# Seven products instead of eight: the MLP of a two-layer encoder by Strassen's scheme, with the sums of weight blocks formed on GpSimd

## The chip, the cores and the metric

The kernel runs on one core of a Trainium2 chip. A core has five engines, each with its own queue of instructions that it takes in order: TensorE (PE, matrix products, with its weight loads shown apart as PEld), VectorE (DVE), ScalarE (ACT), GpSimd (POOL) and SyncE (SP, which here only starts transfers). They wait for each other through semaphores. The metric is the time of one launch on the device in microseconds (us). The kernel before takes 1675.76 us (median of three runs, 1674.79 to 1677.36).

## The reference, cut to what matters

Two layers run over 512 prompt tokens and 32 sample tokens, 544 in all, at width 1024. Each layer has two attention mixers, a cross-attention to 256 memory tokens, and a squared-ReLU MLP of width 4096. The change is about the MLP:

```python
D_MODEL = 1024; D_FF = 4 * D_MODEL; DEPTH = 2
...
def layer(x, pos, l, past, mk, mv):
    mix, rows = mixers(rmsnorm(x, norm_mix[l]), pos, l, past)
    x = x + mix
    x = x + cross_attention(rmsnorm(x, norm_cross[l]), mk, mv, w_xq[l], w_xo[l])
    hm = rmsnorm(x, norm_mlp[l])
    x = x + jnp.square(jax.nn.relu(hm @ w_up[l])) @ w_down[l]
    return x, rows
```

All arithmetic is float32. The products are formed from float32 numbers split into a high and a low part (`wh + wl`, `ah + al`), with three products `wl*ah + wh*ah + wh*al` kept of the four.

## The kernel before

Activations lie in SBUF as features by tokens: `X` [128, 8, 544] is the residual stream, `Ah`/`Al` the two parts of the normed input of a product, `Bh`/`Bl` those of the second product's input. A weight matrix is cut into blocks of 128 output features over 1024 input features ([128, 1024] in SBUF, one transfer of 512 KB each). `split_piece` (lines 208 to 229) makes the two parts of half a block [128, 512]: ScalarE copies it to the rounded type `fp32r` (line 222), and VectorE (even halves) or GpSimd (odd halves) subtracts to get the rest (line 224).

`dense` (line 256) makes one block of outputs: over eight blocks of the contraction, `mm3` (line 246) issues three products for each half of the tokens (272 columns each), so 48 matmuls a block, into one of two PSUM tiles `pd` of two banks. The MLP (in `build`) goes in four groups a layer: eight blocks of `w_up`, then eight blocks of `w_down` that use them. `evac_up` (line 1036) takes a block out of PSUM: VectorE computes max(x, 0) times the norm's factor `R` (line 1039), ScalarE squares it to `Bh` (1040), GpSimd squares it in full (1041), and `rest_up` subtracts on VectorE to `Bl` (1045). `evac_x` (line 986) adds a finished block to `X` on VectorE (line 990) and, in the last group, prepares the next norm with a square on ScalarE and a sum `acc` on GpSimd (line 346). The last two blocks of the second layer go by halves of the tokens (`finish`, `final_norm`).

The order of instructions on each engine comes from a scheduler, which takes the program's order as a priority and may put a later instruction ahead; each engine then keeps that order on the chip. The next block's weights are split while a block's products run.

Of the kernel before, what the change touches and what calls it, by code (L numbers as in the profile page):

```python
# [29 lines left out]
# where in each layer's stream of products the other steps come: after how many of the first blocks' products  # L30
# [11 lines left out]
# norm, and evacuation of the first block that needs it  # L42
NORM = (dict(cross=[8, 11], mlp=(9, 10)),
        dict(cross=(9, 10), mlp=(9, 10)))
# the order of the last outputs: blocks, on GpSimd or not
# [3 lines left out]
# columns of the small constant tables  # L49
# [5 lines left out]
GATE = slice(64, 96)  # L55

# [5 lines left out]
class Program:  # L62
    def __init__(self, ctx, tc, io):
        self.ctx, self.tc, self.nc, self.io = ctx, tc, tc.nc, io
        self.order = []
        self.raw = {}
        self.split = {}
        self.n_loaded = 0
        self.n_split = 0

    # ---------------------------------------------------------------- storage
    def setup(self):
# [13 lines left out]
        # the gains and the first block of the input come in one piece  # L86
# [6 lines left out]
        self.Bl = one.tile([128, KT, NT], F32R, name="Bl")  # L93
        self.Rm = one.tile([128, NMEM], F32, name="Rm")
# [45 lines left out]

    def load_x(self, k):
# [55 lines left out]
    # ---------------------------------------------------------------- weights  # L197
    def load_weights(self, upto):
        while self.n_loaded <= min(upto, len(self.order) - 1):
            i = self.n_loaded  # L200
            ap, pieces, _ = self.order[i]
# [6 lines left out]
    def split_piece(self, i, j):  # L208
        nc = self.nc
        self.load_weights(i)  # L210
        _, pieces, spare = self.order[i]
        out = self.split.setdefault(i, [None] * len(pieces))
        if out[j] is not None:
            return
        n = pieces[j]
# [14 lines left out]

    def split_weights(self, upto, part=None):
        """Splits the weights up to the given block; with part, only that many of the last block's pieces."""
        upto = min(upto, len(self.order) - 1)
        while self.n_split <= upto:
            i = self.n_split
# [1211 lines left out]
```

## Time and profile before

| | |
|---|---|
| median of three runs | 1675.76 us |
| profiled execution, first to last instruction | 1676.7 us |
| TensorE matmuls busy | 1639.7 us (98%), 12543 recorded |
| VectorE, ScalarE, GpSimd busy | 764.5, 695.8, 558.4 us (46%, 41%, 33%) |
| share of TensorE in the chain that ended last | 90% |
| transfers | 157.28 MB, mean 94 GB/s |

The page shows no time of the profiled execution beside its span, so the two first rows are the ones to compare. Busy times are unions: matmuls overlap in the pipeline, so the mean of one (288 ns) is longer than the distance between two. The two MLP stages are the stretches from about 464 to 847 us and from 1285 to 1662 us.

### The profile page before, as it was taken

How to read it: one execution, taken by the hardware profiler on the slowest of the kernel's cores; microseconds unless marked ns; L12 is line 12 of the kernel's file. 1: busy time of each engine (PE TensorE's matmuls, PEld its weight loads, DVE VectorE, ACT ScalarE, POOL GpSimd, SP SyncE). 2: the span in 40 equal slices, each digit the busy share in tenths (PEclk: the TensorE clock that was granted, in tenths of full speed). 3: DMA queues.
4: the chain of work that ended last, by engine and by line, in shares of the span. 5: the costliest groups of instructions: out<-in, count | busy, mean ns of one | idle time of the engine just before them, and what ended most of it. 6: DMA issues, size and time to landing. Idle time of an engine off the chain costs nothing.

```text
span 1676.7 us, 30750 instructions
## 1 busy us (share of the span) xinstructions
PE 1639.7 (98%) x12543; PEld 1554.7 (93%) x12543; DVE 764.5 (46%) x1534; ACT 695.8 (41%) x1429; POOL 558.4 (33%) x500
## 2 busy tenths in 40 slices
PE   8899999999999999999999999999999999999997
PEld 7777889998999999999998778999999999999996
DVE  6956674355442322323358656634554323232233
ACT  6645564444432222223446556544444223232233
POOL 4514232421442322323344223333124323232334
PEclk9899999999999999999999999999999999999998
DMA  4313155221322222222223113542222222222222
GB/s 161 98 42 109 59 167 177 82 83 60 96 89 89 88 89 89 88 89 89 85 81 101 68 52 102 160 157 85 72 68 89 89 88 89 89 89 89 88 89 79
DMA packets 56398, 157.28 MB, mean 94 GB/s; under 512 B 6768, under 2 KB 16048, under 8 KB 56256
## 3 DMA queue, kind: packets, MB, share of 16 engines
q1 hardware_dynamic: 55984, 155.02, 29.6%
q8 instruction: 99, 1.62, 0.4%
q14 instruction: 43, 0.35, 0.1%
q10 hardware_dynamic: 272, 0.28, 0.0%
HBM read 143.49 MB, written 11.75 MB: 93 GB/s over the span
## 4 chain that ended last, share of the span: by engine, by line
PE 90%; DVE 4%; DMA 1%; POOL 1%; issue 0%; ACT 0%; SPq 0%; DVEq 0%; POOLq 0%; ACTq 0%
PE pd L254 76%; PE pt L394 1%; PE S L493 1%; PE S L561 1%; PE pv L588 1%; PE pv L447 1%; PE S L492 1%; PE pv L507 1%; PE S L429 1%; DMA sn<-sin 1%; PE pd L897 1%; PE ph L254 1%; POOL sw L665 1%; PE pt L574 0%; DVE wl L224 0%
## 5 line engine op out<-in xcount | busy, mean ns | idle before, releaser
L222 ACT CAST wh<-raw 128x512 fp32r<-128x512 f32 (+1 forms) x488 | 301.0, 618 | 718.0 <-PE pd L254 673.3
L224 POOL TENSOR_TENSOR wl<-raw,wh 128x512 fp32r<-128x512 f32 (+1 forms) x240 | 311.8, 1300 | 664.3 <-ACT wh L222 455.8
L254 PE MATMUL pd<-Ah,wl 128*128 128x272 f32 (+2 forms) x2032 | 458.8, 297 | 6.3 <-DVE wl L224 3.6
L254 PE MATMUL pd<-Ah,wh 128*128 128x272 f32 (+2 forms) x2032 | 440.1, 288 | 1.0 <-ACT Ah L330 0.8
L254 PE MATMUL pd<-Al,wh 128*128 128x272 f32 (+2 forms) x2032 | 439.3, 287 | 0.1
L254 PEld LDWEIGHTS pd<-Ah,wl 128*128 128x128 f32 (+1 forms) x2032 | 327.9, 189 | 18.5 <-issue 9.4
L254 PEld LDWEIGHTS pd<-Ah,wh 128*128 128x128 f32 (+1 forms) x2032 | 327.9, 189 | 2.4 <-ACT Ah L330 1.9
L254 PE MATMUL pd<-Bh,wl 128*128 128x272 f32 x1568 | 328.8, 290 | 0.9 <-DVE qr L648 0.7
L254 PEld LDWEIGHTS pd<-Al,wh 128*128 128x128 f32 (+1 forms) x2032 | 327.2, 188 | 0.5 <-DVE Al L331 0.5
L254 PE MATMUL pd<-Bh,wh 128*128 128x272 f32 x1568 | 325.8, 288 | 0.0
L254 PE MATMUL pd<-Bl,wh 128*128 128x272 f32 x1568 | 325.2, 288 | 0.0
L254 PEld LDWEIGHTS pd<-Bh,wl 128*128 128x128 f32 x1568 | 246.0, 189 | 3.3 <-issue 1.0
L254 PEld LDWEIGHTS pd<-Bh,wh 128*128 128x128 f32 x1568 | 246.3, 188 | 0.5
L254 PEld LDWEIGHTS pd<-Bl,wh 128*128 128x128 f32 x1568 | 246.2, 188 | 0.3
L990 DVE TENSOR_TENSOR XG<-pd,XG 128x544 f32<-128x544 f32 x94 | 68.2, 725 | 362.0 <-PE pd L254 362.0
L224 DVE TENSOR_TENSOR wl<-raw,wh 128x512 fp32r<-128x512 f32 (+1 forms) x248 | 174.7, 705 | 35.7 <-ACT wh L222 35.1
L1039 DVE SCALAR_TENSOR_TENSOR up<-pd,R 128x544 f32<-128x544 f32 x64 | 46.4, 725 | 171.1 <-PE pd L254 170.9
L1041 POOL TENSOR_TENSOR up<-up 128x544 f32<-128x544 f32 x64 | 70.4, 1100 | 145.8 <-ACT Bh L1040 145.8
L346 POOL TENSOR_TENSOR acc<-acc,sq 128x544 f32<-128x544 f32 x47 | 65.9, 1402 | 122.9 <-ACT sq L345 122.8
L1045 DVE TENSOR_TENSOR Bl<-up,Bh 128x544 fp32r<-128x544 f32 x64 | 46.5, 726 | 74.9 <-POOL up L1041 74.9
L372 ACT ACTIVATE P<-P,nm 128x128 f32<-128x128 f32 (+1 forms) x96 | 54.1, 564 | 38.2 <-DVE nm L370 37.3
L379 DVE TENSOR_SCALAR P<-P,ss 128x128 f32<-128x128 f32 (+3 forms) x144 | 65.0, 451 | 3.8
(276 smaller groups left out, 1551.5 us busy)
## 6 DMA issues: line engine op xcount, KB each, us to landing
raw<-w_up SPq DMA_DIRECT2D x64, 512.0 KB, 3.5
raw<-w_down SPq DMA_DIRECT2D x64, 512.0 KB, 3.5
raw<-w_in SPq DMA_DIRECT2D x28, 512.0 KB, 3.5
raw<-w_mk SPq DMA_DIRECT2D x16, 512.0 KB, 3.7
raw<-w_mv SPq DMA_DIRECT2D x16, 512.0 KB, 3.8
raw<-w_out SPq DMA_DIRECT2D x16, 512.0 KB, 3.6
raw<-w_xq SPq DMA_DIRECT2D x16, 512.0 KB, 3.5
raw<-w_xo SPq DMA_DIRECT2D x16, 512.0 KB, 3.6
```

The lines of the kernel that those rows point to most:

```text
L222: nc.scalar.copy(h[:, :n], r)
L224: eng.tensor_tensor(lo[:, :n], r, h[:, :n].bitcast(F32), ALU.subtract)
L254: nc.tensor.matmul(o, w, a[:, c0:c1], start=start and n == 0, stop=stop and n == 2)
L346: nc.gpsimd.tensor_tensor(self.acc, self.acc, sq, ALU.add)
L372: nc.scalar.activation(P[:, :n], P[:, :n], AF.Exp, bias=nm, scale=-1.0, accum_out=ss)
L379: nc.vector.tensor_scalar(P[:rows, :n], P[:rows, :n], ri[:rows], None, ALU.mult)
L394: nc.tensor.transpose(pt[:, j], P[:, j * 128:(j + 1) * 128], self.ident)
L429: nc.tensor.matmul(ps[:, :w], q[hh][:r, i * 128:n], k[hh][:r, :w], start=m == 0, stop=m == 1)
L990: nc.vector.tensor_tensor(x, ps[:, :, :HALF], x, ALU.add)
L1039: nc.vector.scalar_tensor_tensor(halves(t), ps[:, :, :HALF], 0.0, halves(self.R), ALU.max, ALU.mult)
L1041: nc.gpsimd.tensor_tensor(t, t, t, ALU.mult)
L1045: self.nc.vector.tensor_tensor(self.Bl[:, j], self.up.pop(j), self.Bh[:, j].bitcast(F32), ALU.subtract)
```

## The change

The MLP's two products are done by pairs. In `w_up`, a pair is output block j of the group together with block j + 4; in `w_down`, output block i with block i + 4. The contraction is halved (4 blocks each), and the tokens are halved (272 each). That makes a 2 x 2 by 2 x 2 product of blocks, which Strassen's scheme (in Winograd's form) does with seven products for eight. Each product is 4 contraction blocks by 3 parts, 12 matmuls of 272 columns: 84 a pair, where two blocks took 96.

- Weight side (`split_sum`): of the seven factors three are blocks of weights (`W11`, `W12`, `W22`) and four are sums (`S1` to `S4`), each formed on GpSimd, then split as before by ScalarE and by VectorE or GpSimd (`on_pool`: `S3`, `W12`, `W22` while products of `w_up` are issued, `W12`, `W22` else). A pair has seven splits of [128, 512] where two blocks had four.
- Activation side: `G` holds the four blocks and three sums; `parts` splits them into seven slots for each of the four block pairs (`W7`). For `w_up` this is done once a layer (`wide_a`, `wide_b`, during the products of `w_xo`, whose blocks now come in the order `PAIRED`), for `w_down` in each group by `evac_up`.
- Results add up in PSUM: `PRODUCTS` names for each product its slot and one of three banks X, Z, W. Between the products into X and Z the sums so far are read out: by ScalarE copies (`evac_up`, n < 3), or by VectorE additions into `X` (`evac_down`). Product n + 2 into a bank waits until that reading is done.
- Splits are issued four products ahead (`LOOK`); each pair's two transfers of 512 KB go to one of two sets of buffers.

```diff
+B11, TA, B22, TB, TC, B21, TD = range(7)
+W11, S1, S2, S4, S3, W12, W22 = range(7)
+PRODUCTS = ((B11, "X", True), (TA, "Z", True), (TB, "X", False), (B22, "Z", False), (TC, "X", False),
+            (B21, "W", True), (TD, "X", False))
+HP = 4
+LOOK = 4
...
+    def split_sum(self, i, j):
...
+        (w11, w21), (w12, w22) = [(t[:, :512], t[:, 512:]) for t in self.raw[i]]
+        sums = self.sums.setdefault(i, {})
+        if j in (S1, S2, S3, S4):
+            a, b = {S1: (w21, w22), S2: (sums.get(S1), w11), S4: (sums.get(S2), w12), S3: (w11, w21)}[j]
+            sums[j] = self.p_tile()
+            nc.gpsimd.tensor_tensor(sums[j], a, b, ALU.add)
+            r = sums[j]
+        else:
+            r = {W11: w11, W12: w12, W22: w22}[j]
...
+        h, lo = [pool.tile([128, 512], F32R, tag=tag + x, name="w" + x, bufs=3) for x in "hl"]
+        nc.scalar.copy(h, r)
+        eng = nc.gpsimd if j in self.on_pool else nc.vector
+        eng.tensor_tensor(lo, r, h.bitcast(F32), ALU.subtract)
+        return h, lo
...
+    def pair(self, ap, ops, evac):
...
+        def product(n):
+            slot, bank, first = PRODUCTS[n]
...
+            for i in range(HP):
+                c = slice(i * 128, (i + 1) * 128)
+                ah, al = [self.W7[ops + x][i][:, slot] for x in "hl"]
+                for m, (w, a) in enumerate(((lo, ah), (h, ah), (h, al))):
+                    self.nc.tensor.matmul(st[bank], w[:, c], a, start=first and i == 0 and m == 0,
+                                          stop=i == HP - 1 and m == 2, skip_group_check=True)
...
+    def parts(self, ops, i, s):
+        h, lo = [self.W7[ops + x][i][:, s] for x in "hl"]
+        self.nc.scalar.copy(h, self.G[:, s])
+        self.nc.vector.tensor_tensor(lo, self.G[:, s], h.bitcast(F32), ALU.subtract)
+    def sums_a(self, b12):
+        self.nc.vector.tensor_tensor(self.G[:, TA], self.G[:, B11], b12, ALU.subtract)
+    def sums_b(self, b12):
+        nc, G = self.nc, self.G
+        nc.vector.scalar_tensor_tensor(G[:, TB], G[:, TA], -1.0, G[:, B22], ALU.mult, ALU.subtract)
+        nc.vector.tensor_tensor(G[:, TC], G[:, B22], b12, ALU.subtract)
+    def sums_c(self):
+        nc, G = self.nc, self.G
+        nc.vector.scalar_tensor_tensor(G[:, TD], G[:, TB], -1.0, G[:, B21], ALU.mult, ALU.subtract)
...
-    def evac_up(self, j, ps):
-        nc = self.nc
-        t = self.t_tile("up")
-        nc.vector.scalar_tensor_tensor(halves(t), ps[:, :, :HALF], 0.0, halves(self.R), ALU.max, ALU.mult)
-        nc.scalar.activation(self.Bh[:, j], t, AF.Square)
-        nc.gpsimd.tensor_tensor(t, t, t, ALU.mult)
-        self.up[j] = t
...
+    def evac_up(self, j, n, ps):
...
+        if n < 3:
+            nc.scalar.copy(st[n], ps)
+            return
+        def square(out, x, op, t):
+            nc.vector.scalar_tensor_tensor(out, x, 0.0, r[t], op, ALU.mult)
+            nc.scalar.activation(out, out, AF.Square)
+        if n == 3:
+            b = st[3]
+            nc.vector.tensor_tensor(b, ps, st[2], ALU.add)
+            square(b, b, ALU.max, 1)
+        elif n == 4:
+            nc.vector.tensor_tensor(G[:, B22], ps, st[1], ALU.add)
+            square(G[:, B22], G[:, B22], ALU.min, 1)
+        elif n == 5:
+            nc.vector.tensor_tensor(G[:, B11], ps, st[0], ALU.add)
+            square(G[:, B11], G[:, B11], ALU.max, 0)
+            self.sums_a(st[3])
+            self.parts("B", j, slice(B11, TA + 1))
+        if n == (4 if j == HP - 1 else 5):
+            self.sums_b(st[3])
+            self.parts("B", j, slice(B22, TC + 1))
+        if n == 6:
+            square(G[:, B21], ps, ALU.min, 0)
+            self.sums_c()
+            self.parts("B", j, slice(B21, TD + 1))
+    def evac_down(self, i, goff, n, ps):
...
+        x = self.X[:, i + HP * m, h[t]]
+        nc.vector.tensor_tensor(x, x, ps, op)
...
+            self.on_pool = (S3, W12, W22) if p[3] == "A" else (W12, W22)
+            for z in todo[q:q + LOOK + 1]:
+                self.split_piece(*z)
+            p[1](n)
```

Two places show what this puts on the engines. VectorE first, where the second group of the first layer begins. In the kernel before, the last block of `w_down` (`XG<-pd,XG`) is followed by the first block of `w_up` (`up`, `Bl`), with the splits of weights (`wl`) between:

```order
L990 TENSOR_TENSOR XG<-pd,XG 128x544
L224 TENSOR_TENSOR wl<-raw,wh 128x512
L1039 SCALAR_TENSOR_TENSOR up<-pd,R 128x544
L224 TENSOR_TENSOR wl<-raw,wh 128x512
L1045 TENSOR_TENSOR Bl<-up,Bh 128x544
```

In the changed kernel most of one pair of `w_up` in that group reads so (`pw` and `pd` are the PSUM banks, `e` the parts read out of them, `G` the blocks and their sums, `P` a sum of weights):

```order
L1189 TENSOR_TENSOR e<-pd,e 128x272
L1193 TENSOR_TENSOR G<-pd,e 128x272
L1184 SCALAR_TENSOR_TENSOR e<-e,R 128x272
L1184 SCALAR_TENSOR_TENSOR G<-G,R 128x272
L297 TENSOR_TENSOR wl<-P,wh 128x512
L392 TENSOR_TENSOR G<-G,e 128x272
L397 TENSOR_TENSOR G<-G,e 128x272
L396 SCALAR_TENSOR_TENSOR G<-G 128x272
L1184 SCALAR_TENSOR_TENSOR G<-pd,R 128x272
L388 TENSOR_TENSOR Bl<-G,Bh 128x544
L388 TENSOR_TENSOR Bl<-G,Bh 128x816
L401 SCALAR_TENSOR_TENSOR G<-G 128x272
```

Two blocks of `w_up` had six instructions on VectorE (three each, as above); a pair has eighteen: four splits of weights, eleven of 272 columns, and three `Bl<-G,Bh` of 544, 816 and 544. Of the eleven, four read a PSUM bank and seven read SBUF alone.

GpSimd at the same group's start. Before, it squares (`up<-up`) and takes the odd splits:

```order
L1041 TENSOR_TENSOR up<-up 128x544
L224 TENSOR_TENSOR wl<-raw,wh 128x512 x9
L1041 TENSOR_TENSOR up<-up 128x544
L224 TENSOR_TENSOR wl<-raw,wh 128x512
L1041 TENSOR_TENSOR up<-up 128x544
```

Now, for one pair of `w_up` in that group (`P<-raw` and `P<-P,raw` are the sums of weights):

```order
L288 TENSOR_TENSOR P<-raw 128x512
L297 TENSOR_TENSOR wl<-P,wh 128x512
L288 TENSOR_TENSOR P<-P,raw 128x512 x2
L288 TENSOR_TENSOR P<-raw 128x512
L297 TENSOR_TENSOR wl<-raw,wh 128x512 x2
```

Two blocks of `w_up` had four instructions on GpSimd (two squares, two splits); a pair has seven, all of 512 columns. A pair of `w_down` has six, and two blocks had two. On TensorE the whole program goes from 12294 instructions to 11526.

## Rows read from the trace of the kernel before

**Rows 1.** The page: span, TensorE's busy time, and the chain by engine.
```profile
span 1676.7 us, 30750 instructions
...
PE 1639.7 (98%) x12543; PEld 1554.7 (93%) x12543; DVE 764.5 (46%) x1534; ACT 695.8 (41%) x1429; POOL 558.4 (33%) x500
...
PE 90%; DVE 4%; DMA 1%; POOL 1%; issue 0%; ACT 0%; SPq 0%; DVEq 0%; POOLq 0%; ACTq 0%
```
**Rows 2.** Busy time by stretch: one in each MLP, then two with idle TensorE.
```profile
core 0: us, PE busy (x) PEld busy (x) DVE busy (x) ACT busy (x) POOL busy (x), PEclk, DMA share, GB/s
561.00:658.00 97.00, 97.00 (x778) 97.00 (x777) 28.07 (x41) 25.16 (x40) 30.30 (x25) 1.00 0.29 88
1382.00:1479.00 97.00, 97.00 (x779) 97.00 (x778) 28.10 (x41) 25.17 (x40) 30.24 (x25) 1.00 0.28 88
60.00:80.00 20.00, 15.20 (x100) 13.41 (x100) 16.99 (x43) 13.43 (x32) 9.28 (x7) 0.92 0.52 157
1665.00:1677.00 12.00, 0.72 (x2) 0.30 (x2) 5.75 (x11) 1.35 (x3) 3.24 (x4) 0.61 0.54 186
```
**Rows 3.** Timeline of VectorE: start, length (us), instruction, idle before; one block of `w_up`.
```profile
499.36 0.72 DVE L1039 SCALAR_TENSOR_TENSOR up<-pd,R 128x544 f32<-128x544 f32 x1 [2.65 <-PE pd L254]
500.06 0.69 DVE L224 TENSOR_TENSOR wl<-raw,wh 128x512 fp32r<-128x512 f32 x1
501.99 0.73 DVE L1045 TENSOR_TENSOR Bl<-up,Bh 128x544 fp32r<-128x544 f32 x1 [1.24 <-POOL up L1041]
505.36 0.72 DVE L1039 SCALAR_TENSOR_TENSOR up<-pd,R 128x544 f32<-128x544 f32 x1 [2.65 <-PE pd L254]
```
**Rows 4.** Groups by line and shape: count, busy us, mean ns, idle before.
```profile
L224 POOL TENSOR_TENSOR wl<-raw,wh 128x512 fp32r<-128x512 f32 x235 | 306.5, 1305 | 638.6 <-ACT wh L222 433.6 <-issue 172.8 <-DMA raw<-w_down 9.4
L222 ACT CAST wh<-raw 128x512 fp32r<-128x512 f32 x476 | 294.9, 621 | 708.7 <-PE pd L254 665.3 <-DMA raw<-w_mv 13.2 <-issue 12.5
L346 POOL TENSOR_TENSOR acc<-acc,sq 128x544 f32<-128x544 f32 x47 | 65.9, 1402 | 122.9 <-ACT sq L345 122.8
L1040 ACT ACTIVATE Bh<-up 128x544 fp32r<-128x544 f32 x64 | 42.3, 661 | 9.1 <-DVE up L1039 3.3
L396 ACT COPY PT<-pt 128x384 f32<-128x384 f32 x48 | 22.7, 474 | 15.6 <-PE pt L394 15.3
```
**Rows 5.** Timeline of VectorE, then of GpSimd, where the first MLP begins.
```profile
467.04 0.73 DVE L323 SCALAR_TENSOR_TENSOR R<-lt,R 128x544 f32<-128x544 f32 x1
469.36 0.72 DVE L1039 SCALAR_TENSOR_TENSOR up<-pd,R 128x544 f32<-128x544 f32 x1 [0.77 <-PE pd L254]
471.13 1.59 DVE L224 TENSOR_TENSOR wl<-raw,wh 128x512 fp32r<-128x512 f32 x1
...
467.06 1.86 POOL L224 TENSOR_TENSOR wl<-raw,wh 128x512 fp32r<-128x512 f32 x1 [4.12 <-ACT wh L222]
469.36 1.10 POOL L1041 TENSOR_TENSOR up<-up 128x544 f32<-128x544 f32 x1 [0.45 <-ACT Bh L1040]
470.92 1.25 POOL L1041 TENSOR_TENSOR up<-up 128x544 f32<-128x544 f32 x1 [0.46 <-ACT Bh L1040]
```
**Rows 6.** The same near the end of the program, instructions of 272 columns.
```profile
1661.09 0.44 DVE L322 SCALAR_TENSOR_TENSOR lt<-lt,R 128x272 f32<-128x272 f32 x1
1661.57 0.90 DVE L323 SCALAR_TENSOR_TENSOR R<-lt,R 128x272 f32<-128x272 f32 x1
...
1661.30 0.87 POOL L1008 TENSOR_TENSOR acc<-acc,sqf 128x272 f32<-128x272 f32 x1 [6.16 <-ACT sqf L1006]
```
**Rows 7.** Timeline of ScalarE near the end: a square of 272 columns.
```profile
1660.79 0.43 ACT L1006 ACTIVATE sqf<-XG 128x272 f32<-128x272 f32 x1 [0.27 <-DVE XG L1004]
```
**Rows 8.** The page: transfers of the MLP's weights, KB each, us to landing.
```profile
raw<-w_up SPq DMA_DIRECT2D x64, 512.0 KB, 3.5
raw<-w_down SPq DMA_DIRECT2D x64, 512.0 KB, 3.5
```

More of the change, by code (lines that the diff above doesn't have):

```diff
@@ L200, in load_weights @@
             i = self.n_loaded
-            ap, pieces, _ = self.order[i]
+            ap, pieces, spare = self.order[i]
+            if spare == "pair":
+                pool, tag = ((self.wraw, "raw"), (self.mlp_pool, "mraw"))[self.n_pair % 2]
+                self.n_pair += 1
+                self.raw[i] = [pool.tile([128, 1024], F32, tag=tag, name="raw", bufs=2) for _ in range(2)]
+                for j in range(2):
+                    self.nc.sync.dma_start(out=self.raw[i][j], in_=ap[j])
+                self.n_loaded += 1
+                continue
             n = sum(pieces)
@@ L209, in split_piece @@
         nc = self.nc
+        if (i, j) in self.done:
+            return
+        self.done.add((i, j))
         self.load_weights(i)
@@ L261, in dense, with step @@
         st = {}
-        def step(k, part=range(2)):
-            if k == 0 and part[0] == 0:
+        ks = ks or range(kt)
+        def step(k):
+            first, last = k == ks[0], k == ks[-1]
+            if first:
                 if ahead:
@@ L1270, in build @@
                     t.append(self.now)
[L1271 to L1272 removed]
+            xo = [self.dense(io["w_xo"][l, m], 128, *B, bind(self.evac_x, m, G_MLP + 8 * l), ahead=int(n != 1))
+                  for n, m in enumerate(PAIRED)]
             xo2 = len(self.order) - 6
@@ L1282, in build @@
                          for h in range(4)], t[3] + 8.4)
+            self.then([(0, lambda g=g: self.wide_b(3, g))])
             goff = G_MIX + 8 if l == 0 else G_FIN
+            prods, ends = [], {}
             for grp in range(4):
-                up = [self.dense(io["w_up"][l, 8 * grp + j], 128, *A, bind(self.evac_up, j)) for j in range(8)]
-                if grp == 0:
-                    up[0], up[1] = behind(up[0], up[1], self.norm, *NORM[l]["mlp"])
-                n = 6 if l == L - 1 and grp == 3 else 8
@@ L1290, in build @@
-                down = [self.dense(io["w_down"][l, grp, m], 128, *B, bind(self.evac_x, m, goff if grp == 3 else None))
-                        for m in range(n)]
-                jobs = up + down
-                for j in range(8):
-                    jobs[j + 1] = at(jobs[j + 1], 5 if grp == 0 and j == 0 else 3, self.rest_up, j)
-                for j in jobs:
-                    self.then(j)
-        self.pn = {}
-        w = []
-        def extra(j):
-            if not w:
-                self.last_ctx, p = self.pool("last", "left")
-                w.extend([p.tile([128, 512], F32R, name=f"{n}{i}") for n in ("lh", "ll")] for i in range(2))
-            return w[j]
@@ L1307, in build @@
-        a0, a1 = self.dense(io["w_down"][L - 1, 3, 6], 128, *B, lambda j, ps: self.finish(6, j, ps), turns=self.ps_t)
-        b0, b1 = self.dense(io["w_down"][L - 1, 3, 7], 128, *B, lambda j, ps: self.finish(7, j, ps), turns=self.ps_s,
-                            spare=extra)
-        b0 = at(b0, 7, self.final_sum, 0)
-        a1 = at(a1, 6, self.final_norm, 0)
-        b1 = at(b1, 7, self.final_sum, 1)
-        for j in (a0, b0, a1, b1):
-            self.then(j)
-        self.then([(0, lambda: self.final_norm(1)), (0, lambda: self.last_ctx.close())])
+                up = [self.pair(io["w_up"][l, grp, j], "A", bind2(self.evac_up, j)) for j in range(4)]
@@ new lines, in build @@
+                down = [self.pair(io["w_down"][l, grp, i], "B", bind2(self.evac_down, i, goff if grp == 3 else None))
+                        for i in range(4)]
+                pairs = up + down
+                p = [[(x, n) for n in range(7)] for x in pairs]
+                if grp == 0:
+                    p[0], p[1] = p[0][:2] + p[1][:2], [("norm", None)] + p[0][2:] + p[1][2:]
+                p[3], p[4] = p[3][:4] + p[3][5:6] + p[3][4:5] + p[4][:1], p[3][6:] + p[4][1:]
+                if l == L - 1 and grp == 3:
+                    p[6], p[7] = p[6][:5] + p[7][:5], p[6][5:] + p[7][5:]
```

191 lines of the change are left out of this document (146 added, 45 removed).

## The prediction

> **What bounds the kernel now.** I read the page first: TensorE is busy 1639.7 of 1676.7 us and makes 90% of the chain that ended last [rows 1]. Then the busy times of a stretch in each MLP [rows 2]: TensorE is busy in all of 97.00 us, with 778 matmuls, so one matmul costs 97.00/778 = 0.1247 us; VectorE has 28, ScalarE 25 and GpSimd 30 us of work in the same 97. Then VectorE's timeline through one block of `w_up` [rows 3]: two evacuations begin at 499.36 and 505.36, so a block takes 6.00 us (48 x 0.1247 = 5.99). Two blocks take 12.0 us, and the others have two thirds of that free. Last I looked for VectorE and GpSimd instructions that touch in time [rows 5, 6], since the change fills just these two queues.
>
> **What the change takes away.** There are 2 layers x 4 groups x 8 = 64 pairs, half of `w_up`, half of `w_down`. Each has 84 matmuls instead of 96, so 768 go, which is what the order of TensorE's instructions shows too. At TensorE's pace a pair then takes 84 x 0.1247 = 10.5 us instead of 12.0, and the whole 768 x 0.1247 = 96 us less. The pace itself should hold: matmuls have the same 272 columns, and before the change each already has its own weight load (12543 of both [rows 1]), so nothing is lost when two neighbours no longer share weights.
>
> **What it adds, by engine, for a pair of `w_up`.** Durations: a split's copy on ScalarE 0.62, its difference on GpSimd 1.30 [rows 4] and on VectorE 0.69 [rows 3]; 272 columns take VectorE 0.44 [rows 6] and ScalarE's square 0.43 [rows 7]; a 384-column copy out of PSUM takes 0.47 [rows 4], so I estimate 0.39 for 272. From 0.44 at 272 and 0.73 at 544 [rows 3, 6] I estimate 1.02 for 816 on VectorE, and 0.93 on ScalarE with its 0.66 for 544 [rows 4].
> - ScalarE: 7 x 0.62 + 3 x 0.39 + 4 x 0.43 + 0.66 + 0.93 + 0.66 = 9.5 us.
> - VectorE: 4 x 0.69 + 11 x 0.44 + 0.73 + 1.02 + 0.73 = 10.1 us.
> - GpSimd: 7 x 1.30 = 9.1 us; a sum of 512 columns is in no row, and the addition of 544 at 1.40 [rows 4] says about 1.3 for it.
>
> Each alone would just fit beside TensorE's 10.5 us. But VectorE and GpSimd do not run beside each other freely. In [rows 5] a GpSimd difference begins at 467.06 just behind a VectorE instruction (467.04 to 467.77) and takes 1.86 instead of 1.30: it ends 1.15 behind it. A VectorE split that begins at 471.13, while GpSimd works from 470.92 to 472.17, takes 1.59 instead of 0.69 and ends 0.55 behind it. In [rows 6] one of 272 columns takes 0.90 instead of 0.44, ending 0.30 behind GpSimd. An evacuation with one input in PSUM runs beside a GpSimd square at 469.36 at its usual 0.72, and the square at its usual 1.10. So the two take turns wherever VectorE reads two operands from SBUF, and only the first 0.14 us of whoever waits is hidden. The turn costs GpSimd 1.15 per instruction of 512, and VectorE 0.55, 0.59, 0.88 or 0.30 at 512, 544, 816 and 272.
>
> The Trainium skill says the same in "SBUF — State Buffer", section "Who interferes with whom": a VectorE instruction with two SBUF inputs and a GpSimd instruction that reads SBUF exclude each other, and the second blocks until the first has finished. The trace agrees (1.59 for 0.69), except that 0.14 us is hidden; by the page's words alone a pair of `w_up` would need at least 9.1 + 8.3 = 17.4 us, an estimate with whole durations, and the kernel some 1840.
>
> Of VectorE's 18 instructions four read PSUM (the three additions and one scaling); 14 must take turns with GpSimd's seven.
> - At least: 7 x 1.15 + 4 x 0.55 + 7 x 0.30 + 0.59 + 0.88 + 0.59 = 14.4 us a pair, if every start and every PSUM instruction hides behind GpSimd.
> - At most, with no further waits: VectorE's own 10.1 plus seven turns of 1.15, 18.1 us.
>
> VectorE keeps its order, so its work is a sum: each GpSimd instruction pushes it back by 1.15, unless it lies beside a PSUM instruction (four of 0.44). I take three of these four as covered: 18.1 - 1.3 = 16.8 us. TensorE can't run ahead of that: products into X wait until ScalarE and VectorE have read the bank (an addition on `pd` must be done before the pair's seventh product), and the next pair's weights are subtracted in the same VectorE queue. Behind each VectorE instruction that waits stand those very additions, and TensorE waits for them. 32 pairs x (16.8 - 12.0) = +154 us.
>
> **A pair of `w_down`.** GpSimd has 6 x 1.30 = 7.8, VectorE five splits that take turns and seven additions with PSUM that do not: 3.45 + 3.1 = 6.5; ScalarE 4.3. Turns: 6 x 1.15 + 5 x 0.55 = 9.65 us, under TensorE's 10.5. GpSimd's queue from end to end is at most 7.8 + 5 x 0.55 = 10.6, as long as TensorE's, plus waits for ScalarE's copies that I can't read from any row: between 10.5 and 12. I take 11.0, near TensorE's own. 32 x (11.0 - 12.0) = -32 us.
>
> **Smaller parts.** In each layer's last group GpSimd also gets eight additions of 1.40 (as before), on a queue that is now full: 16 x 1.26 = up to 20 us, I take 16. `wide_a` and `wide_b` add some 2.4 us of VectorE and ScalarE work for every two blocks of `w_xo`, which have 12 us; VectorE's turns and GpSimd's there come to 10.7, so that is hidden, except the last `wide_b` (about 6 us behind the last block, against 4 products of 1.5 us ahead of the one that needs it). That, the changes between `w_up` and `w_down`, and the last outputs I put at +6, between 0 and 15. The transfers are the same bytes; a pair's two take some 3.5 us each [rows 8] and have a pair's whole time, so nothing.
>
> **Sum.** Against the profiled 1676.7 us: + 154 - 32 + 16 + 6 = +144, so 1821. The median of the runs is 0.9 lower: 1820 us.
>
> **Rivals.**
> - *TensorE stays the bound.* For it: no single engine has more than 10.1 us of work in 10.5. Then 96 us go: 1580. With some loss in the loop through the banks (VectorE from the W bank's end to the sum in slot `TA`, 7 x 0.44 + 2 x 0.69 = 4.5; ScalarE then five instructions up to the next copy out of X, 0.66 + 0.62 + 0.93 + 0.43 + 0.39 = 3.0; TensorE 30 matmuls, 3.7, until W is done again: 11.2, with hand-overs about 11.4 a pair of `w_up`) it would be 1676.7 - 32 x 0.6 - 32 x 1.5 = 1610. Either is a faster kernel. Against it: the rows on turns; a pair of each kind must fall under 24.0 us together, and 14.4 + 10.5 is 24.9. It decides if turns between the new small instructions cost much less than the 0.30 and 1.15 read here. 0.09.
> - *The turns at their least.* The scheduler's order happens to put GpSimd's work beside VectorE's waits and PSUM instructions: 32 x (14.4 - 12.0) - 32 x 1.5 = +29, with the smaller parts 1705 to 1745. 0.14.
> - *Everything waits.* No PSUM instruction is covered, `w_down` is held by GpSimd at 12.0, the smaller parts at their upper ends: 32 x 6.1 + 20 + 15 = +230: 1906. TensorE would then be busy 60% of a pair of `w_up`; the granted clock read 0.92 where it was busy 15.2 of 20 us, and 0.61 only where it had next to nothing to do [rows 2], so the clock should add little. 0.09.
> - *No change.* The losses just meet the 96 us: only between the first two cases. 0.02.
>
> That the change doesn't do what it says is ruled out by the order: the 768 matmuls are gone.
>
> **How the numbers follow.** The forecast, 1745 to 1885, has 0.66. The range of 1710 to 1885 leaves out below it the faster kernel, no change and the lowest times of the least case (0.12 together), and above it nearly all of the last case (0.08). Slower by over 0.2% (what a measurement of this kernel can tell from no change) are forecast, least and everything: 0.66 + 0.14 + 0.09 = 0.89; faster 0.09; within 0.2% 0.02.
>
> **What would show it.** Right: in the MLP TensorE's busy share falls to about two thirds in the stretches of `w_up` and stays near full in those of `w_down`; VectorE's splits of 512 columns have a mean well over 0.69 there and GpSimd's instructions over 1.30; a pair of `w_up` takes 16 to 17 us from one to the next; the longest waits of TensorE name VectorE or ScalarE in lines of `evac_up`. Wrong: VectorE's instructions keep 0.44 and 0.69 while GpSimd is busy; or pairs of `w_up` follow each other at 10.5 us, or wait for ScalarE or transfers instead.

## The result and the profile after

The changed kernel takes 1940.68 us (median of 4 runs, 1936.74 to 1946.31) against 1675.74: ratio 1.1582 [1.1561, 1.1602]. The forecast was 1820 with a range up to 1885: the sign was right, the size was not, 121 us are missing. The page of the kernel after, its span, busy times and the chain that ended last (before: [rows 1]):

```profile
span 1934.8 us, 30761 instructions
...
PE 1678.8 (87%) x11775; PEld 1550.4 (80%) x11775; DVE 1286.9 (67%) x2196; ACT 912.2 (47%) x1909; POOL 924.8 (48%) x732
...
PE 25%; DVE 11%; POOL 6%; ACT 2%; issue 2%; DMA 1%; POOLq 0%; ACTq 0%; DVEq 0%; SPq 0%
```

The 768 matmuls are gone (11775 for 12543), and TensorE's share of the chain falls from 90% to 25%. To split the MLP into its pairs I took VectorE's first read of the tile `pw` in each pair: there is one a pair, in the lines of `evac_up` and `evac_down`. From one such read to the next group's is a stretch of four pairs. Busy time by stretch of the kernel after, columns as in [rows 2], first four pairs of `w_up`, then four of `w_down`:

```profile
600.20:667.61 67.41, 50.43 (x338) 46.79 (x338) 61.10 (x76) 32.96 (x66) 38.37 (x28) 0.92 0.18 62
667.61:726.65 59.04, 48.71 (x337) 46.79 (x336) 27.50 (x44) 17.50 (x32) 35.71 (x26) 0.91 0.21 73
```

A pair of `w_up` takes 67.41/4 = 16.85 us (forecast 16.8). A pair of `w_down` takes 59.04/4 = 14.76 (forecast 11.0, with 12 as the upper bound). A group of eight pairs was forecast at 4 x 27.8 = 111.2 us and takes 126.45, so 15.25 us more. This is one of the longer groups: the six that can be read so (all but the last of each layer) take 119.6 to 127.1, 123.9 in the mean, and 12.7 us more in each of eight groups make some 100 of the 121 us.

How a group's miss divides between `w_up` and `w_down` depends on the cut, for `pw` is read inside a pair, not at its end: the first stretch above ends inside the first pair of `w_down`, the second inside a pair of `w_up`. Cut instead at the read of each pair's last product (`G<-pd,R` in `w_up`, the seventh addition to `XG` in `w_down`), the same group reads:

```profile
587.83:659.60 71.77, 51.44 (x337) 47.51 (x336) 57.23 (x71) 32.02 (x66) 40.53 (x30) 0.91 0.17 59
659.60:714.15 54.55, 47.85 (x338) 46.22 (x339) 31.10 (x49) 18.45 (x32) 33.28 (x24) 0.93 0.23 78
```

So a pair of `w_up` takes 17.9 us and one of `w_down` 13.6. By either cut the larger part of the miss, 10.6 to 15 us of a group's 15.25, lies in `w_down`; by the second, 4.6 us are `w_up`'s. The pairs of single runs below are cut at `pw`, as in the first table. No engine is full in `w_down`: VectorE and GpSimd have 27.5 and 35.7 of 59 us. The waits of TensorE over the whole program say where it stands (what waits, for what, us in total, times, longest):

```profile
PE pw L379 <- POOL wl L297: 120.1, 45, 6.7
PE pd L379 <- ACT e L1180: 35.3, 25, 3.1
PE pd L379 <- DVE G L1193: 26.1, 21, 3.0
```

The first is product 5 of a pair, the one in a bank of its own (`pw`), waiting for the small part of `W12`, whose difference is on GpSimd. It is not `w_down`'s alone. Of matmuls that read `Ah` (`w_up`), then of those that read `Bh` (`w_down`), these waited for it:

```profile
  POOL wl L297: 69.4, 22
  POOL wl L297: 50.7, 23
```

One such wait in a pair of `w_down`, on TensorE and then on GpSimd:

```profile
689.27 0.39 PE L379 MATMUL pw<-Bh,wl 128*128 128x272 f32 x1 [2.98 <-POOL wl L297]
...
685.02 1.28 POOL L288 TENSOR_TENSOR P<-raw 128x512 f32<-128x512 f32 x1
686.27 2.95 POOL L297 TENSOR_TENSOR wl<-raw,wh 128x512 fp32r<-128x512 f32 x2
693.17 1.31 POOL L288 TENSOR_TENSOR P<-raw 128x512 f32<-128x512 f32 x1 [3.95 <-DVE wl L297]
```

TensorE goes on 0.05 us after the second of the two differences (686.27 + 2.95), which is `W12`'s: GpSimd's order has `W22`'s ahead of it. GpSimd then idles 3.95 us, until VectorE has freed a buffer of sums: an engine that is late is also idle.

That the turns are real can be read inside this one kernel. The same line of `evac_up`, once with two operands in SBUF and once with one in PSUM (count: shortest/median/longest, ns):

```profile
L1184 DVE SCALAR_TENSOR_TENSOR G<-G,R x64: 426/1166/1550, 478.8 to 1866.0; 128x272 f32<-128x272 f32 x64
L1184 DVE SCALAR_TENSOR_TENSOR G<-pd,R x32: 427/428/443, 483.1 to 1870.2; 128x272 f32<-128x272 f32 x32
```

The operation and the size are the same; from SBUF the median is 1166 ns, from PSUM 428. GpSimd's difference takes 1443 ns here for 1305 in [rows 4]; of its sums, those that read an earlier sum take 1479:

```profile
L288 POOL TENSOR_TENSOR P<-P,raw 128x512 f32<-128x512 f32 x128 | 189.3, 1479 | 48.0 <-DVE wl L297 43.1
L297 POOL TENSOR_TENSOR wl<-raw,wh 128x512 fp32r<-128x512 f32 x128 | 183.2, 1443 | 59.9 <-ACT wh L295 59.1
```

### The profile page after: what moved, and what is told of

Its sections match the earlier page's. It is cut to its first block, busy times and chain, and to the rows that moved or that the text cites. A ratio compares the mean times of both kernels' runs of the same rounds, so it can differ in the third digit from the quotient of the medians.

```text
span 1934.8 us, 30761 instructions
## 1 busy us (share of the span) xinstructions
PE 1678.8 (87%) x11775; PEld 1550.4 (80%) x11775; DVE 1286.9 (67%) x2196; ACT 912.2 (47%) x1909; POOL 924.8 (48%) x732
## 5 line engine op out<-in xcount | busy, mean ns | idle before, releaser
L379 PE MATMUL pd<-Ah,wl 128*128 128x272 f32 x768 | 250.7, 327 | 70.9 <-ACT e L1180 35.3
L288 POOL TENSOR_TENSOR P<-raw 128x512 f32<-128x512 f32 x128 | 172.7, 1349 | 269.9 <-DVE wl L297 119.6
L327 PE MATMUL pd<-Ah,wl 128*128 128x272 f32 (+2 forms) x1008 | 247.7, 306 | 5.4 <-DVE wl L273 3.7
L379 PE MATMUL pd<-Bh,wl 128*128 128x272 f32 x768 | 237.6, 312 | 13.2 <-DVE wl L297 6.3
L379 PE MATMUL pd<-Ah,wh 128*128 128x272 f32 x768 | 239.7, 312 | 0.0
L379 PE MATMUL pd<-Al,wh 128*128 128x272 f32 x768 | 236.9, 312 | 0.0
L379 PEld LDWEIGHTS pd<-Ah,wl 128*128 128x128 f32 x768 | 164.1, 214 | 90.0 <-ACT e L1180 48.7
L327 PE MATMUL pd<-Ah,wh 128*128 128x272 f32 (+2 forms) x1008 | 229.3, 288 | 1.0 <-ACT Ah L460 0.9
L297 DVE TENSOR_TENSOR wl<-P,wh 128x512 fp32r<-128x512 f32 x216 | 189.7, 887 | 60.5 <-ACT wh L295 60.0
L327 PE MATMUL pd<-Al,wh 128*128 128x272 f32 (+2 forms) x1008 | 228.8, 288 | 0.2
L288 POOL TENSOR_TENSOR P<-P,raw 128x512 f32<-128x512 f32 x128 | 189.3, 1479 | 48.0 <-DVE wl L297 43.1
L297 POOL TENSOR_TENSOR wl<-raw,wh 128x512 fp32r<-128x512 f32 x128 | 183.2, 1443 | 59.9 <-ACT wh L295 59.1
```

The lines of the kernel that those rows point to most:

```text
L288: nc.gpsimd.tensor_tensor(sums[j], a, b, ALU.add)
L297: eng.tensor_tensor(lo, r, h.bitcast(F32), ALU.subtract)
L327: nc.tensor.matmul(o, w, a[:, c0:c1], start=start and n == 0, stop=stop and n == 2)
L379: self.nc.tensor.matmul(st[bank], w[:, c], a, start=first and i == 0 and m == 0, stop=i == HP - 1 and m == 2, skip_group_check=True)
```

## The experiments

**First theories: a loop through buffers, GpSimd's rate, the clock, the turns.** Four runs beside each other. e1, one line of `mlp`:

```
-            self.on_pool = (S3, W12, W22) if p[3] == "A" else (W12, W22)
+            self.on_pool = (S3, W12, W22) if p[3] == "A" else ()
```

> Edit: in the pairs of w_down the differences of W12 and W22 go from GpSimd to VectorE; w_up is untouched. Theory A (loop): a pair of w_down lasts 14.3 to 15 us because product 5 waits for W12's difference, which stands on GpSimd behind four sums that wait for their buffers, which wait for VectorE's differences of the pair before, for ScalarE's copies, for weight buffers and so for TensorE again. With the differences on VectorE, GpSimd has four sums of about 1.29 us in a pair and the loop opens: the pair falls to 10.9 to 11.5 us, near TensorE's 10.5, and the kernel to 1820 to 1860 us; the wait of product 5 for wl on GpSimd is gone from the trace. Theory B (clock): the pair is long since TensorE has a lower granted clock (0.91) after every pause; then the pair stays above 13.5 us and the time above 1900 us. Pairs of w_up stay at 16.7 us in both.

1878.44 us, 1.1206 [1.1163, 1.1249]. Its stretches of `w_up` and of `w_down`:

```profile
591.92:659.23 67.31, 52.66 (x326) 49.46 (x327) 58.99 (x76) 32.52 (x65) 34.98 (x26) 0.85 0.17 57
659.23:709.09 49.86, 46.41 (x349) 44.09 (x347) 32.26 (x52) 18.05 (x32) 26.62 (x19) 1.00 0.27 87
```

A pair of `w_down` falls to 12.5 us, not to 11: GpSimd's place in the chain of `w_down` is worth 62 us (its wait in front of `pw` falls from 120.1 to 61.6 us, all of that in `w_up`), and something else holds the pair above TensorE's 10.5.

e2, in `split_sum`, two of the four sums from another ring of buffers (`self.down` holds the pairs of `w_down`):

```
-            sums[j] = self.p_tile()
+            sums[j] = self.t_tile("P", 512) if i in self.down and j in (S2, S3) else self.p_tile()
```

> Edit: in the pairs of w_down two of the four weight sums take buffers of another ring (five deep, unused there), so that the ring of four serves two pairs instead of one; engines and operations are as in the changed kernel. Theory A (loop through the sums' buffers): GpSimd's 4 to 5 us of idle time in a pair, which end with VectorE's difference of the same sum one pair earlier, go away; W12's difference comes sooner, the pair falls from 14.3-15 to 11 to 12 us, the kernel to 1840 to 1880 us. Theory A2 (only the place of W12's difference behind four sums in GpSimd's order): the idle time moves elsewhere, the pair stays above 13.5 us and the kernel at 1915 to 1945 us.

1921.03 us, 1.1468 [1.1409, 1.1527]; the pair still takes (725.62 - 669.56)/4 = 14.0 us. The loop through the sums' buffers was my first theory, and it fell as the main cause: more buffers are worth 20 us, and the wait in front of `pw` stays (89.9 us).

e3, no sums in `w_down` (the output changes):

```
+            if i in self.down:
+                sums[j] = {S1: w21, S2: w22, S4: w12, S3: w21}[j]
+            else:
...
```

> Edit: in the pairs of w_down the four weight sums are left out; the raw blocks W21, W22, W12, W21 are split in their place (so the output changes); seven products and all splits stay. Theory A (loop): GpSimd has only two differences of 1.3 to 1.7 us in a pair and nothing waits for a sum; the pair comes to 10.6 to 11.2 us and the kernel to 1805 to 1840 us. Theory B (clock, or the splits' other waits): the pair stays at 13 us or more, the kernel at 1890 us or more.

1843.45 us, 1.0986 [1.094, 1.1033]; a pair takes (707.15 - 653.46)/4 = 13.4 us up to the next group's first `pw`. Inside the group the pairs follow at 11.7, 11.8 and 13.2 us; the change to `w_up` makes the rest. `w_down`'s sums are worth 97 us, a part of it in `w_up` (four pairs 63.96 us for 67.41), but even without any sum the pair does not come to 10.5. So the sums alone do not explain it.

e4, no GpSimd work in the MLP's weights at all:

```
-            sums[j] = self.p_tile()
-            nc.gpsimd.tensor_tensor(sums[j], a, b, ALU.add)
-            r = sums[j]
+            r = sums[j] = {S1: w21, S2: w22, S4: w12, S3: w21}[j]
...
-            self.on_pool = (S3, W12, W22) if p[3] == "A" else (W12, W22)
+            self.on_pool = ()
```

> Edit: in the pairs of w_up and w_down the weight sums are left out (raw blocks are split in their place, so the output changes) and all seven differences of a pair are on VectorE: GpSimd has no work in these stages. Theory T (turns: a VectorE instruction with two operands in SBUF waits while GpSimd works): VectorE's own work in a w_up pair falls from 15.2 us busy to about 12 in spite of three more differences, since the 512-wide difference is back at 0.69 us and the 272-wide at 0.44; the w_up pair comes to 11.8 to 12.6 us, the w_down pair to 10.6 to 11, and the kernel to 1650 to 1690 us. Rival (VectorE's durations don't depend on GpSimd): the 512-wide difference stays at 1.09 us and the 272-wide at 1.09, the w_up pair grows to 17 to 18 us, the kernel stays above 1800 us.

1668.12 us, 0.993 [0.9907, 0.9954]. Stretches of `w_up` and `w_down`, then the line that took 1166 ns:

```profile
561.52:608.26 46.74, 43.99 (x327) 41.69 (x328) 43.06 (x87) 32.63 (x66) 0.00 (x0) 1.00 0.28 84
608.26:654.59 46.33, 45.82 (x348) 44.05 (x346) 28.82 (x56) 17.75 (x32) 0.00 (x0) 1.00 0.31 99
```
```profile
L1182 DVE SCALAR_TENSOR_TENSOR G<-G,R x64: 429/433/436, 475.0 to 1606.0; 128x272 f32<-128x272 f32 x64
```

VectorE does three more differences a pair of `w_up` and is busy 43.1 us instead of 61.1. The same instruction takes 433 ns again, never over 436. This settles the turns: they, and not VectorE's own work, make VectorE slow in `w_up`. (The edit takes away TensorE's waits for GpSimd too; but VectorE was busy 61.1 of 67.41 us there.) The Trainium skill's rule in "SBUF — State Buffer", section "Who interferes with whom" (a VectorE instruction with two SBUF inputs and a GpSimd instruction that reads SBUF exclude each other) agrees with these rows. But the pairs take 11.7 and 11.6 us here, and the time is only 0.7% under that of the kernel before. Even free of turns, the pair did not reach the 10.5 us of its matmuls.

**The order of TensorE's instructions.** Since neither load nor buffers held `w_down`, I read TensorE's order in the changed kernel, one row of each product of a pair of `w_down`. By the numbers at `wl` the program's order is 7648 (`W11`), 7667 (`S1`), 7686 (`S2`), 7706 (`S4`), 7725 (`S3`), 7743 (`W12`), 7760 (`W22`); 7627 is the pair before:

```
3220 L379 MATMUL pd_7728<-Bh_88,wl_7648 128x272
...
3244 L379 MATMUL pd_7595<-Bh_88,wl_7627 128x272
...
3256 L379 MATMUL pd_7728<-Bh_88,wl_7667 128x272
...
3268 L379 MATMUL pw_7822<-Bh_88,wl_7743 128x272
...
3273 L379 MATMUL pd_7728<-Bh_88,wl_7686 128x272
...
3286 L379 MATMUL pw_7822<-Bh2_5106,wl_7743 128x272
...
3290 L379 MATMUL pd_7728<-Bh_88,wl_7706 128x272
...
3307 L379 MATMUL pd_7728<-Bh_88,wl_7725 128x272
```

The scheduler begins product 5 (`pw`, `W12`) between products 1 and 2: TensorE asks for `W12`'s part ahead of `S2`, `S4` and `S3`, three products before its place in the program (the expectation below says four), while GpSimd makes it behind four sums. e5 holds TensorE to the program's order (an order without a wait); e6 adds e1's line:

```
...
+                    with self.tc.issue_after(self.last_mm) if self.last_mm else nullcontext():
+                        mm = self.nc.tensor.matmul(st[bank], w[:, c], a, start=first and i == 0 and m == 0,
+                                                   stop=i == HP - 1 and m == 2, skip_group_check=True)
+            self.last_mm = mm.ins
```

> Edit: in the MLP TensorE's instructions are held to the program's order, product by product (an order without a wait); nothing else is asked for. In the changed kernel the scheduler sets the first products with W12 (the ones into the tile pw) between S1's and S2's, S4's, four products before their place in the program, so TensorE asks for W12's split when it has just used S1's. Theory A3 (the place of W12's product in TensorE's order, not the ring of sum buffers, is what makes a pair of w_down wait): the waits of pw for wl on GpSimd (120 us in all in the changed kernel) fall below 30 us, a pair of w_down falls from 14.5 to 11.5 to 12.5 us, pairs of w_up stay at 16 to 17 (VectorE's turns), the kernel comes to 1840 to 1880 us. Rival (GpSimd's six instructions of 1.3 to 1.7 us with their turns set the pair, in any order): the pair stays at 13.5 us or more, the kernel above 1910 us; the wait moves to another product.

> Edit: TensorE held to the program's order in the MLP as in the run beside it, and in w_down the differences of W12 and W22 on VectorE. By A3 the pair of w_down is then TensorE's own: 10.8 to 11.8 us, the kernel 1815 to 1850 us. By the rival (GpSimd's rate) the run without the order, 1878 us with 12.5 us a pair, can't be much improved: 1865 to 1885 us.

1971.21 us, 1.1764 [1.1735, 1.1792], and 1968.65, 1.1741 [1.172, 1.1762]: slower than the changed kernel. Both theories fell as they were put. But the two runs agree: the wait for GpSimd is gone, and another has come that does not care who makes the difference. Stretches of `w_up` and `w_down` in e5:

```profile
605.50:680.90 75.40, 50.58 (x317) 47.63 (x316) 57.13 (x75) 31.89 (x62) 39.31 (x28) 0.82 0.18 56
680.90:734.80 53.90, 47.62 (x358) 45.03 (x357) 33.01 (x47) 19.71 (x35) 33.75 (x25) 1.00 0.23 79
```

`w_down` is shorter than in the changed kernel (53.9 us for 59.0); `w_up` (75.4 for 67.4) makes these runs the slower ones. TensorE in e5 at a change of product in `w_down`, then VectorE:

```profile
702.52 0.29 PE L381 MATMUL pd<-Bl,wh 128*128 128x272 f32 x1
703.34 0.39 PE L381 MATMUL pd<-Bh,wl 128*128 128x272 f32 x1 [0.53 <-DVE XG L1218]
...
700.56 0.44 DVE L1218 TENSOR_TENSOR XG<-XG,pd 128x272 f32<-128x272 f32 x1
701.25 0.69 DVE L298 TENSOR_TENSOR wl<-P,wh 128x512 fp32r<-128x512 f32 x1 [0.26 <-ACT wh L296]
702.84 0.44 DVE L1218 TENSOR_TENSOR XG<-XG,pd 128x272 f32<-128x272 f32 x1 [0.90 <-PE pd L381]
```

Between two products 0.82 us pass instead of 0.125, and the first matmul takes 0.23 us to the next instead of 0.125: some 0.8 us are lost, three times a pair, and 10.5 + 3 x 0.8 = 12.9 us is just the distance of e6's pairs inside a group (12.9). The next product waits for VectorE's addition of an earlier one, and that addition for TensorE. The compiled program says why: `X` and `Z` are the two banks of one PSUM tile (`pd`), and the addition of product n stands behind product n+1 in the program. So the addition of product 1 (in `Z`) waits for the end of product 2 (in `X`) too, and product 3 for that addition: a false wait. The scheduler had filled these pauses with product 5. The same tile makes ScalarE's copies in `w_up` (`evac_up`) wait too, and TensorE for them (149.1 us in e5).

**A tile each.** e7 gives `Z` a PSUM tile of its own, e8 adds the program's order, e9 adds e1's line:

```
-                d = self.ps_d.tile([128, 2, 512], F32, tag="d", name="pd")
-                st["X"], st["Z"] = d[:, 0, :HALF], d[:, 1, :HALF]
+                st["X"] = self.ps_d.tile([128, 2, 512], F32, tag="d", name="pd")[:, 0, :HALF]
+                st["Z"] = self.ps_s.tile([128, 512], F32, tag="s", name="pz")[:, :HALF]
```

> Edit: the two accumulators X and Z of a pair, which share one PSUM tile of two banks, get a tile each (Z from the norm's pool); TensorE's order is the scheduler's again. Theory F (false wait): with one tile, VectorE's evacuation of product n waits for the end of product n+1 too, and product n+2 for that evacuation; held to the program's order TensorE pauses 0.79 us three times in a pair of w_down (12.9 us with either engine for W12's difference), and it is to fill these pauses that the scheduler sets W12's product early. With a tile each the order becomes the program's but for one matmul of pw that still stands before S2's. By F and A3 together (that one matmul still asks for W12 early) the pair of w_down is 12.5 to 14 us and the kernel 1850 to 1915 us. Rival (GpSimd's rate): 14 us and 1915 to 1945.

> Edit: a tile each for X and Z, and TensorE held to the program's order; GpSimd keeps W12's and W22's differences in w_down. Theory F: no pause after evacuations and no early W12; the pair of w_down is 10.8 to 11.8 us, pairs of w_up 16 to 17 us (VectorE with its turns), the kernel 1800 to 1850 us, 120 to 170 us less than with the program's order and one tile (1971). Rival (it is VectorE's evacuation standing behind blocked differences that stops TensorE, whatever the tile): the pair stays at 12.5 us or more and the kernel above 1920.

> Edit: as the run beside it (a tile each, program's order), and W12's and W22's differences of w_down on VectorE. Theory F: TensorE's bound again, 10.7 to 11.5 us for a pair of w_down, the kernel within 20 us of the run beside it, since then neither engine is the bound there (GpSimd 5.2 or 9.9 us of 10.5). By the rival (GpSimd's rate) this run is 80 us or more below the run beside it.

1906.19 us, 1.1354 [1.1326, 1.1382]; 1874.0, 1.1165 [1.1146, 1.1183]; 1835.29, 1.0938 [1.089, 1.0985]. Stretches of `w_down` in e7, e8 and e9:

```profile
676.80:724.75 47.95, 42.97 (x335) 41.98 (x335) 34.17 (x49) 18.86 (x33) 34.26 (x23) 1.00 0.20 66
```
```profile
665.65:714.32 48.67, 43.69 (x342) 42.75 (x340) 33.12 (x48) 19.49 (x34) 35.74 (x24) 1.00 0.19 65
```
```profile
662.36:706.37 44.01, 42.51 (x336) 41.93 (x335) 36.06 (x54) 18.80 (x33) 25.16 (x17) 1.00 0.29 91
```

e7's time is as expected, its pair (12.0 us) a little shorter; e8's is 24 us above the expectation, its pair 12.2. In e9 the pair is 11.0 us, the forecast's own number, and TensorE is busy 42.5 of 44.0. The false wait is shown: with the order held, a tile each is worth 97 us (1971 to 1874), and more of it in `w_up` (four pairs 75.4 to 67.1 us) than in `w_down` (53.9 to 48.7). GpSimd's part is shown too, against e9's expectation of 20 us: with two differences more on GpSimd the pair is 12.2 us, and the kernel 39 us slower. No single edit does it: the tile alone gives 35 us, the order alone loses 30, the engine alone gives 62, all three 105.

**What was left.** e14 holds the order in `w_down` only:

```
-                    with self.tc.issue_after(self.last_mm) if self.last_mm else nullcontext():
+                    with self.tc.issue_after(self.last_mm) if self.last_mm and ops == "B" else nullcontext():
```

> Edit: the changed kernel with a tile each for X and Z, W12's and W22's differences of w_down on VectorE, and TensorE held to the program's order in w_down alone: w_up is left to the scheduler as in the changed kernel. Theory: w_down's pair (10.8 us once its order and tiles are right) is the whole of what the forecast missed, so that the forecast's own sum returns: 1940 less 32 x 3.5, 1810 to 1840 us, pairs of w_up at 15.5 to 17 us. Rival (the order in w_up costs what is left between 1835 and 1820): the pairs of w_up fall by 0.5 us or more and the time to 1790 to 1815 us.

1864.53 us, 1.1103 [1.1081, 1.1124], above both. Its stretches of `w_up` and `w_down`:

```profile
585.90:657.80 71.90, 52.40 (x337) 50.29 (x336) 62.00 (x75) 32.79 (x64) 40.01 (x28) 0.83 0.20 68
657.80:701.55 43.75, 43.07 (x339) 42.49 (x339) 35.11 (x55) 18.79 (x33) 25.70 (x17) 1.00 0.26 82
```

`w_down` is right again (10.9), but a group takes 115.65 us against e9's 112.51: a part of what `w_down` gains is given back in `w_up`. With a tile each, holding `w_up`'s order too gains 29 us (e9). With the order left to the scheduler, `w_up` again has the wait for GpSimd in front of `pw`: 62.2 us in e14, 82 us in e7's `w_up`, none in e9. How much of the difference that makes was not separated. e12 takes GpSimd's work out of `w_up` alone, on top of e9 (the sums are left out there, and all differences are on VectorE):

```
-            sums[j] = self.p_tile()
-            nc.gpsimd.tensor_tensor(sums[j], a, b, ALU.add)
+            if i in self.down:
+                sums[j] = self.p_tile()
+                nc.gpsimd.tensor_tensor(sums[j], a, b, ALU.add)
+            else:
+                sums[j] = {S1: w21, S2: w22, S4: w12, S3: w21}[j]
...
-            self.on_pool = (S3, W12, W22) if p[3] == "A" else (W12, W22)
+            self.on_pool = ()
```

> Edit on the version with a tile each, the program's order and w_down's differences on VectorE (1835 us, pairs of w_up 17.1, of w_down 10.8 us): in w_up alone the weight sums are left out (raw blocks are split in their place, so the output changes) and all differences are on VectorE, so that GpSimd has nothing to do in w_up's stretches and VectorE 1.3 us of differences more for each pair than GpSimd gave up. Theory T (turns): VectorE's work falls to about 12 us for a pair in spite of the added differences, pairs of w_up come to 11.5 to 13 us and the kernel to 1650 to 1710 us. Rival (w_up is bound by its chain through ScalarE's copies and VectorE's evacuations, not by the turns): pairs of w_up stay at 15 us or more and the kernel above 1770 us.

1743.39 us, 1.0401 [1.0383, 1.0419]. The stretch of two pairs of `w_up` inside a group, and the one from its last pair to the first of `w_down`:

```profile
573.06:595.54 22.48, 22.33 (x178) 22.12 (x177) 22.03 (x43) 16.62 (x34) 1.72 (x2) 1.00 0.29 94
609.96:630.90 20.94, 15.53 (x107) 14.81 (x106) 18.73 (x26) 8.99 (x16) 8.25 (x6) 0.84 0.17 53
```

The first two pairs of a group take 11.2 us in the mean, TensorE full: the turns again. The time is above the expectation all the same, for I missed the end of the group: the third pair takes 14.4 us, and at the change to `w_down` TensorE, in the program's order, waits for the last block's parts, so that this one interval takes 20.9.

**A version that beats both.** e10 takes the seven products where they pay: `w_up` dense as before, `w_down` as in e9 with deeper rings.

```
+                up = [self.dense(io["w_up"][l, 8 * grp + m], 128, *A, bind(self.evac_up, m)) for m in PAIRED]
...
+            h, lo = [self.mlp_pool.tile([128, 512], F32R, tag="mw" + x, name="w" + x, bufs=7) for x in "hl"]
```

> A version that may beat both kernels: w_up is done by dense products as in the kernel before (its pairs of blocks 12.0 us of matmuls, VectorE and GpSimd with room), the seven products only in w_down, with a tile each, the program's order, all differences of w_down on VectorE, and deeper rings in the room that the parts of A leave. By theory F w_down's pair is 10.7 to 11.5 us against 12.0: 16 to 42 us less over 32 pairs, against some 5 to 10 us at the eight changes from w_up to w_down (the sums of the last block) and at the end: 1640 to 1670 us. Rival (turns and evacuations hold the pair at 12.5 us or more): 1690 us or more.

1669.16 us (7 runs), 0.9945 [0.9924, 0.9966]: 0.55% faster than the kernel before, at the upper end of what was expected. Its pairs of `w_down` take 10.7 to 10.9 us in most groups and a group 92.1 us against some 96. The first three groups of each layer gain 24 us together, but 8.4 are lost again ahead of the first MLP, in the stage of `w_xo`, where the first sums were set ahead of `w_xo`'s differences, and 10.6 from the last group of layer 0 to the start of the second MLP, which I did not take apart. e11 holds all sums and transfers to the program's place, e13 those of the first pair in each layer; in both the split of `X` also stands ahead of its square, and in e11 `w_xo`'s blocks go in the order 0 to 7 again. e13's line for the sums:

```
-            nc.gpsimd.tensor_tensor(sums[j], a, b, ALU.add)
+            s = nc.gpsimd.tensor_tensor(sums[j], a, b, ALU.add)
+            if i in self.early:
+                self.tc.keep_in_program_order(s)
```

> Edit on the version with dense w_up and seven products in w_down only: the transfers of w_down's blocks and GpSimd's weight sums keep their place in the program (without it the scheduler sets the sums of the first pairs, and their transfers, into the stage of w_xo, where w_xo's differences stand behind them and TensorE loses some 9 us in layer 0 and 5 in layer 1); w_xo's blocks go 0 to 7 and the split of x ahead of its square, as in the kernel before. The stage before the MLP should then run as before: 10 to 14 us less than 1669, 1655 to 1660 us, 1.0 to 1.2% under the kernel before. If the loss there has another cause (the opening of the MLP's storage), no change: 1666 to 1672.

> Edit on the version with dense w_up and seven products in w_down only (1669 us): only the first pair of w_down in each layer has its transfers and sums held to their place in the program (and the split of x stands ahead of its square). If GpSimd's sums and SP's transfers set into w_xo's stage are what costs TensorE 9 and 5 us there, and holding every sum (1740 us) cost by putting the sums of each group beside VectorE's sums of the activations, this gives 1653 to 1664 us; if the loss in w_xo's stage has another cause, 1666 to 1674; if the place of the first group's sums alone costs as holding all did, its eighth to quarter of 71 us, 1678 or more.

1740.2 us, 1.0384 [1.0364, 1.0405], and 1674.02 (11 runs), 0.9978 [0.9966, 0.999]. Both missed. In e13 the stage of `w_xo` is whole (first row e10, second e13), and the loss has moved to the first change from `w_up` to `w_down` (third row, e13):

```profile
430.00:460.00 30.00, 24.84 (x177) 24.63 (x178) 18.04 (x17) 11.66 (x21) 19.53 (x13) 0.89 0.37 111
430.00:460.00 30.00, 30.00 (x240) 30.00 (x240) 10.63 (x16) 12.90 (x21) 13.26 (x10) 1.00 0.27 79
490.00:520.00 30.00, 22.78 (x155) 22.02 (x154) 25.15 (x32) 13.86 (x26) 17.55 (x12) 0.83 0.40 129
```

There the sums meet VectorE's sums of the activations, which must take turns with them (one of 272 columns takes 1.54 us); e11 pays this in every group, some 9 us each. So in these two runs the scheduler's early sums were not a mistake. e10 stays the best.

## Why the prediction was right and wrong

- *TensorE's saving* (84 matmuls, 10.5 us a pair): the count and the pace were right, and e9's 11.0 and e10's 10.7 to 10.9 come near it. But a pair reaches it only with its accumulators apart and TensorE in the program's order.
- *Turns, a pair of `w_up`*: the mechanism was right. e4 and e12 show it by taking GpSimd away: 11.7 and 11.2. The size was right within 7% (16.85 us by one cut, 17.9 by the other, for 16.8; that the first meets it so closely is luck), but in part by another way: 69.4 us of TensorE's waits in `w_up` are for GpSimd's `W12`, which the working does not have. In e9, where these are gone, TensorE waits for `evac_up`, as forecast (`PE pd L381 <- ACT e L1183: 80.3, 20, 4.8`), and the pair still takes 17.1.
- *A pair of `w_down`*: this is the step that failed. It said that GpSimd's queue from end to end is at most 10.6 us, as long as TensorE's, with 10.5 to 12 as the bounds. The sum of the queue was about right (GpSimd is busy 35.7/4 = 8.9 us a pair), but a queue is no chain. Which product asks for GpSimd's result, and when, stood in TensorE's order, from which the forecast took only the count of matmuls. The order puts `W12` three products early, because of the tile that `X` and `Z` share (with a tile each, in e7, 13.4 of the 50.7 us of this wait are left in `w_down`); neither was in the working. By the two cuts the pair is 2.6 to 3.8 us above 11.0, over 32 pairs 85 to 120 us; e9, with the tile, the order and the engine changed, gives the 11.0.
- *The smaller parts* (+16 and +6): not seen apart. The groups make some 100 of the 121 us, so that about 20 lie in the last group of each layer and at the ends, where these parts are.
- *The rivals*: "everything waits" had `w_down` at 12.0 as the worst. A bound that is built from one engine's own work is no upper bound where two engines wait for each other.
- *Signs named beforehand*: VectorE's and GpSimd's longer instructions came. TensorE's longest waits name GpSimd's `wl` and only behind it lines of `evac_up`; TensorE is busy 75% in `w_up` instead of two thirds, and in `w_down` 83% instead of near full: the first and the last pointed to the failed step at once.
- *The clock*: the forecast let it add little. The granted clock reads 0.91 in `w_down` and 1.00 in e1, e5 and e9, where TensorE pauses less or more briefly; in `w_up` it reads 0.92, and 0.82 in e5. It follows the waits; what it costs by itself was not separated (a bound is in the last section).

## What to carry to other kernels

Where a change saves matmuls by adding small work on other engines, first ask which of the added operations read SBUF twice on VectorE while GpSimd works; then read TensorE's order, product by product, and ask for each operand who makes it and how far ahead. Two accumulators that are evacuated in turn belong into two PSUM tiles: in one tile each evacuation can wait for the other's products. A scheme that saves matmuls need not be used everywhere: here it pays in `w_down` and costs in `w_up`.

## What was not expected of the hardware

TensorE's clock fell in a pause that a wait made, and the pause was paid for a second time. In e10's stage of `w_xo` TensorE waited 4.04 us for a difference on GpSimd, up to 441.40. Busy times ahead of that wait, behind it, and later:

```profile
430.00:436.90 6.90, 5.78 (x46) 5.78 (x47) 6.82 (x6) 4.04 (x8) 6.74 (x5) 1.00 0.47 154
441.40:446.50 5.10, 5.10 (x22) 5.10 (x23) 0.53 (x1) 0.00 (x0) 2.98 (x2) 0.50 0.58 144
447.00:452.00 5.00, 5.00 (x42) 5.00 (x42) 2.81 (x3) 2.54 (x4) 2.57 (x2) 1.00 0.06 25
```

Behind the wait the granted clock is 0.50 (1.2 GHz) for 5.1 us and TensorE does 22 matmuls, 0.23 us each; later it is 1.00 (2.4 GHz) with 0.12 each. So the wait of 4.04 us cost some 2.4 us more. In the kernel after, a mean of 0.91 in `w_down` means that 18% of 59.04 us were at the lower level, so the clock is at most 5.3 of the 15 us which four pairs, cut at `pw`, take too long (an estimate); the forecast had put it at little.
